# Sixteen-by-sixteen triangle inverses moved from VectorE to GpSimd, with five block transfers per chain in place of eighteen

## The chip, the cores and the metric

The kernel runs on one core of a Trainium2 chip. The metric is the device time of one execution in microseconds (us). Names of engines in the profile: PE is TensorE (matmuls), PEld its weight loads, DVE is VectorE, ACT is ScalarE, POOL is GpSimd, and SP (SPq) is the engine that issues most of the DMAs.

## The reference, cut to what matters

Two layers, each a half-step feed-forward block, a mixing block and another half-step feed-forward block, on 512 tokens of width 1024. The mixing block runs three groups of heads side by side on one projection: attention over a sliding window, RWKV-7 and a short convolution.

```python
proj = hn @ w_mix_in[l]
p_att, p_rwkv, p_conv = jnp.split(proj, [...], axis=-1)
y_att  = sliding_window_sink_attention(p_att, ...)      # 8 query heads, window 128
y_rwkv = rwkv7_time_mix(p_rwkv, ...)                    # 4 heads of 64
y_conv = short_conv_mix(p_conv, conv_w[l])
h = h + (1.0 + gt2) * (jnp.concatenate([y_att, y_rwkv, y_conv], -1) @ w_mix_out[l])

# RWKV-7, one head: a state S of 64 x 64, updated token by token
def step(S, inp):
    r_t, w_t, k_t, v_t, kk_t, a_t = inp
    s_kk = jnp.einsum('bhvk,bhk->bhv', S, kk_t)
    S = (S * w_t[:, :, None, :] - s_kk[..., None] * (kk_t * a_t)[:, :, None, :]
         + v_t[..., None] * k_t[:, :, None, :])
    return S, jnp.einsum('bhvk,bhk->bhv', S, r_t)
```

## The kernel before, in words

**The frame.** A layer is the feed-forward block, the mixing block, the feed-forward block. Weights stream from DRAM; each chunk is split into a high and a low part (a cast on ACT at L101, a subtraction on DVE at L102) and multiplied in three matmuls (L98 in the mixing block). The L98 matmuls of the mixing block, 128x256 each, are the projections in and out. They depend on little else, so they serve as the work that PE does while the small steps of the heads wait.

**The chains.** The four RWKV heads are two chains, `rwkv(0)` and `rwkv(1)`, of two heads each; a chain keeps its two heads on the 128 partitions. It replaces the token loop by chunks of 64 tokens (CH = 64). Each chunk of each head needs the inverse of a unit lower triangular 64x64 matrix, and a chain has 16 of them (2 heads, 8 chunks):

1. PE makes the products `ps_c` from `AR` and `a` (L824), and DVE masks them into the tile `B` in two instructions (L828). `LT`, a part of `B`, holds the transposed triangles.
2. The 16x16 diagonal blocks (BASE = 16, four in each 64x64 block, 64 per chain) are gathered, one block to a partition. This goes through DRAM: one transfer writes `LT` to `dl` (L836), eight read the blocks back into `G` (L846).
3. The blocks are inverted by elimination: GpSimd sets `inv` to the identity (two memsets, L848 and L849), then 15 steps follow, of two DVE instructions each: a product into `elim` (L853) and a subtraction from `inv` (L854), on 64 partitions and 15 to 64 elements per partition. Each instruction needs the result of the one before it.
4. The inverted blocks go back through DRAM: one transfer writes `di` (L856), eight read it into `C` (L859).
5. DVE spreads `C` into the block diagonal tile `T` (L907) and transposes it into `TT` (L908). Two levels of 64x64 matmuls on PE (`ps_x`, `ps_t`, `ps_tt`, L916), with masks and subtractions on DVE between them, join the blocks to the inverse of the whole triangle.
6. The rest of the chain (`ps_w`, `ps_gn`, `ps_o`, `ps_s`, `ps_ys`) uses that inverse and runs the state over the chunks.

Between steps 2 and 5 the chain has work that doesn't need the inverse: products `ps_c` from `AR` and `iP` for the tile `K` (L824, L828), the transposes `ps_vN`, `ps_ta`, `ps_beN`, `ps_kaN` (L867) and `ps_xv` (L893).

**The order of the work.** The projections (`products()`), `rwkv(0)`, `rwkv(1)` and `attention()` are generators. A loop at the end of the mixing block takes one step of each that is alive and pays the L98 matmuls out against it by credits, from three totals that are written by hand: `RWKV_WORK, ATT_WORK, FILL_WORK = 29.8, 15.2, 129.6` (L34); the numbers behind `yield` are the costs. From the program written in this way a scheduler fixes the order of the instructions of each engine before the kernel runs. On the chip each engine takes its list in that order, and an instruction that waits holds up all behind it on the same engine. The DMAs of `dl`, `G`, `di` and `C` are issued by SP, from the same list as the weight loads (`wraw`, L267).

Of the kernel before, what the change touches and what calls it, by code (L numbers as in the profile page):

```python
# [8 lines left out]
F32 = mybir.dt.float32  # L9
# [3 lines left out]
ALU = mybir.AluOpType  # L13
# [3 lines left out]
P = 128  # L17
# [8 lines left out]
NB = T // P  # L26
CH = 64
NC = T // CH
HB = math.exp(-0.5) / 2
BASE = 16  # L30
# [27 lines left out]
def trunk_kernel(ctx, tc, ins, out, layers=L, phases=("ffn1", "mix", "ffn2")):  # L58
    nc = tc.nc
# [10 lines left out]
    dram = ctx.enter_context(tc.tile_pool(name="dram", bufs=1, space=bass.MemoryType.DRAM))  # L70
    tt, stt, ts = nc.vector.tensor_tensor, nc.vector.scalar_tensor_tensor, nc.vector.tensor_scalar
    act, mm = nc.scalar.activation, nc.tensor.matmul

    def E(name="e", dt=F32):
        return sp.tile([P, T], dt, name=name, tag="e", bufs=4)
# [34 lines left out]
    rows = (slice(0, CH), slice(CH, P))  # L110
# [7 lines left out]
    for i in range(KD):  # L118
        t = hp_.tile([P, T], F32, name=f"h{i}")
# [15 lines left out]
    for name, v in (("eps", EPS), ("eps64", 64 * EPS), ("gneps", GN_EPS), ("nhb", -HB)):  # L135
        t = const.tile([P, 1], F32, name=f"v_{name}")
# [71 lines left out]
    def square(i, sl):  # L208
        sq = E("sq")[:, sl]
        act(sq, h[i][:, sl], AF.Square)  # L210
        return sq
# [373 lines left out]
    def mix(l, hn, ss, mp, then, ready):  # L585
# [5 lines left out]
        def pair(name):  # L591
            return rows_of(name != "y4", (name + "H", name + "L"))

        def S(q, name, shape=(P, T)):
            return mp.tile(list(shape), F32, name=f"{name}{q}", tag=f"s{q}", bufs=8)
# [4 lines left out]
        def EQ(q, name):  # L600
            return mp.tile([P, T], F32, name=name, tag=f"e{q}", bufs=2)
# [154 lines left out]
        def rwkv(q):  # L756
# [38 lines left out]
            t = EQ(q, "k2")  # L795
# [36 lines left out]
            B_, other = yield from pairs(be, "B", other)  # L832
            LT = B_[:, :, :, 0]

            dl = dram.tile([P, 2 * NB, CH], F32, name="dl", tag=f"dl{q}", bufs=2)
            nc.sync.dma_start(dl, LT.rearrange("p e b t -> p (e b) t"))  # L836
            NM = CH // BASE
            NT = 2 * NM * 2 * NB
            square = lambda t: t[:NT, : BASE * BASE].rearrange("p (t u) -> p t u", u=BASE)
            G = square(EQ(q, "G"))  # L840
            for c in range(2):
                for m in range(NM):
                    n = (c * NM + m) * 2 * NB
                    p0 = c * CH + m * BASE
                    src = dl[p0 : p0 + BASE, :, m * BASE : (m + 1) * BASE]
                    nc.sync.dma_start(G[n : n + 2 * NB], src.rearrange("r n t -> n r t"))  # L846
            V_ = square(EQ(q, "inv"))
            nc.gpsimd.memset(V_, 0.0)  # L848
            nc.gpsimd.memset(V_.rearrange("p t u -> p (t u)")[:, :: BASE + 1], 1.0)  # L849
            for s in range(BASE - 1):  # L850
                n = BASE - 1 - s
                t = mp.tile([NT, BASE * BASE // 4], F32, name="elim", tag=f"el{q}")[:, : n * (s + 1)].rearrange("p (t u) -> p t u", u=s + 1)
                tt(t, G[:, s, s + 1 :].unsqueeze(2).to_broadcast([NT, n, s + 1]), V_[:, s : s + 1, : s + 1].to_broadcast([NT, n, s + 1]), ALU.mult)  # L853
                tt(V_[:, s + 1 :, : s + 1], V_[:, s + 1 :, : s + 1], t, ALU.subtract)  # L854
            di = dram.tile([2 * NM, 2 * NB, BASE, BASE], F32, name="di", tag=f"di{q}", bufs=2)
            nc.sync.dma_start(di.rearrange("m n t u -> (m n) t u"), V_)  # L856
            C_ = EQ(q, "C")[:, : 2 * NB * BASE].rearrange("p (n u) -> p n u", u=BASE)
            for m in range(2 * NM):
                nc.sync.dma_start(C_[m * BASE : (m + 1) * BASE], di[m].rearrange("n t u -> t n u"))  # L859


            AX = U(q, "AX", [P, 2, NB, 2, CH])
# [80 lines left out]
            with tc.manual_schedule(engines={mybir.EngineType.PE}):  # L943
                for b in range(NB):
                    for c, e in ce:
                        m = mm(pgs[c][rows[e], 0, b], Wn[rows[c], e, b, :CH], beN[rows[c], b, rows[e]], start=True, stop=True)
# [12 lines left out]
            y = S(q, "y")  # L959
            pos = [psum([P, 2, NB, CH], "ps_o", R) for _ in range(2)]  # L960
            with tc.manual_schedule(engines={mybir.EngineType.PE}):
                for b in range(NB):
                    for c, e in ce:
                        m = mm(pos[c][rows[e], 0, b], Wn[rows[c], e, b, :CH], B_[rows[c], e, b, 1], start=True, stop=True)
# [116 lines left out]

        prod = products()
        live, waiting = {}, {"rwkv0": lambda: rwkv(0), "rwkv1": lambda: rwkv(1), "att": attention}
        left, fill, credit = 2 * RWKV_WORK + ATT_WORK, FILL_WORK, 0.0
        more = True
# [28 lines left out]
        for q in range(2):  # L1114
            x = pair("yr")
# [256 lines left out]
```

## Time and profile before

| what | before |
|---|---|
| time, median of 3 runs | 1912.6 us (1911.94 to 1915.08) |
| the profiled execution's own time | 1913.21 us |
| its span in the trace | 1911.2 us |
| mean granted clock of TensorE | 0.996 of full speed |
| PE busy | 1878.8 us of the span |
| DVE busy | 1399.8 us |
| ACT busy | 837.0 us |
| POOL busy | 130.7 us |
| the mixing chains' `dl` transfers issued at | 479.21 and 522.88 us (layer 1), 1415.64 and 1459.31 us (layer 2) |

The profile shows one execution; its own time is 0.6 us over the median. The span is what the trace covers, and 2.0 us of the execution lie around it. In rows of groups the columns are the line, the engine, the operation, the tile written and the tile read, the shapes and the count, then the busy time in us, the mean duration of one in ns and the idle time before them, with what ended it. In rows of the timeline the first number is the start in us and the second the length of the row's work; a bracket at the end is the time that the engine sat idle before it, and what ended that.

### The profile page before, as it was taken

The numbers are of one execution on the slowest core, as the hardware profiler recorded it, in microseconds if no ns is written. First come the engines' busy times: TensorE is split into PE (matmuls) and PEld (weight loads), VectorE is DVE, ScalarE is ACT, GpSimd is POOL, SyncE is SP. The second block draws the span as 40 slices with busy tenths as digits, with TensorE's granted clock in tenths as the row PEclk, the third lists the DMA queues.
The fourth block names the chain that finished last, engine by engine and source line by source line (L and its number), as shares of the span: only waits on it lengthen the run. The fifth ranks groups of instructions, "written<-read, shape, count | busy, mean of one in ns | idle before, by whom it ended". The sixth has DMA issues, their size and how long they took to land. (4 is left out here: it accounts for less than half of the span.)

```text
span 1911.2 us, 37042 instructions
## 1 busy us (share of the span) xinstructions
PE 1878.8 (98%) x15504; PEld 1741.7 (91%) x15504; DVE 1399.8 (73%) x2181; ACT 837.0 (44%) x1264; POOL 130.7 (7%) x212
## 2 busy tenths in 40 slices
PE   8999999999999999999999999999999999999999
PEld 7998899897888999899899989989878899988998
DVE  7687687758976877677877776876599667864862
ACT  4443255346322554155345514544562235532551
POOL 0101100100000001110100020010000000110000
PEclk8999999999999999999999999999999999999999
DMA  7767877521312476887727678781321315774741
GB/s 300 245 168 221 271 198 229 168 70 45 79 43 81 123 198 176 278 218 199 264 62 193 171 260 242 191 278 42 93 61 49 88 34 163 209 217 130 198 140 59
DMA packets 104326, 308.46 MB, mean 161 GB/s; under 512 B 23392, under 2 KB 24416, under 8 KB 103136
## 3 DMA queue, kind: packets, MB, share of 16 engines
q1 hardware_dynamic: 75936, 203.33, 32.9%
q0 software_dynamic: 28224, 102.77, 21.7%
q8 instruction: 121, 1.98, 0.4%
q14 instruction: 45, 0.37, 0.1%
HBM read 302.66 MB, written 3.41 MB: 160 GB/s over the span
## 5 line engine op out<-in xcount | busy, mean ns | idle before, releaser
L101 ACT CAST wH<-wraw 128x1024 fp32r<-128x1024 f32 (+2 forms) x292 | 268.4, 922 | 512.6 <-PE ps_mm L91 176.8
L102 DVE TENSOR_TENSOR wL<-wraw,wH 128x1024 fp32r<-128x1024 f32 (+2 forms) x292 | 308.1, 1058 | 96.9 <-ACT wH L101 95.8
L90 PE MATMUL ps_mm<-actH,wH 128*128 128x512 f32 (+1 forms) x784 | 288.5, 368 | 0.0
L91 PE MATMUL ps_mm<-actL,wH 128*128 128x512 f32 (+1 forms) x784 | 288.0, 367 | 0.0
L92 PE MATMUL ps_mm<-actH,wL 128*128 128x512 f32 (+1 forms) x784 | 288.0, 367 | 0.0
L441 PE MATMUL ps_d<-comH,wH 128*128 128x256 f32 x816 | 226.8, 278 | 1.6 <-ACT wH L101 0.8
L443 PE MATMUL ps_d<-comH,wL 128*128 128x256 f32 x816 | 225.8, 277 | 2.3 <-DVE wL L102 2.3
L442 PE MATMUL ps_d<-comL,wH 128*128 128x256 f32 x816 | 225.5, 276 | 0.0
L98 PE MATMUL ps_mm<-hnH,wH 128*128 128x256 f32 x1040 | 214.0, 286 | 5.1 <-ACT hnH L101 2.9
L98 PE MATMUL ps_mm<-hnL,wH 128*128 128x256 f32 x1040 | 211.8, 283 | 0.0
L98 PE MATMUL ps_mm<-hnH,wL 128*128 128x256 f32 x1040 | 209.5, 281 | 0.5 <-DVE wL L102 0.5
L163 DVE SCALAR_TENSOR_TENSOR wada<-wada,crep 128x1024 f32<-128x1024 f32 x140 | 168.0, 1220 | 47.8 <-DMA wada<-in_wadaT 47.6
L102 DVE TENSOR_TENSOR wL<-sum,wH 128x1024 fp32r<-128x1024 f32 x102 | 124.8, 1224 | 74.9 <-ACT wH L101 74.7
L98 PEld LDWEIGHTS ps_mm<-hnH,wH 128*128 128x128 f32 x1040 | 159.5, 190 | 16.1 <-issue 8.2
L92 PEld LDWEIGHTS ps_mm<-actH,wL 128*128 128x128 f32 x784 | 147.8, 189 | 24.4
L90 PEld LDWEIGHTS ps_mm<-actH,wH 128*128 128x128 f32 x784 | 147.8, 189 | 24.2
L91 PEld LDWEIGHTS ps_mm<-actL,wH 128*128 128x128 f32 x784 | 147.8, 189 | 24.1
L101 ACT CAST wH<-sum 128x1024 fp32r<-128x1024 f32 x102 | 107.5, 1054 | 140.3 <-PE ps_d L442 60.1
L98 PEld LDWEIGHTS ps_mm<-hnL,wH 128*128 128x128 f32 x1040 | 160.2, 190 | 6.7 <-issue 5.7
L98 PEld LDWEIGHTS ps_mm<-hnH,wL 128*128 128x128 f32 x1040 | 160.1, 190 | 4.1 <-issue 2.9
L441 PEld LDWEIGHTS ps_d<-comH,wH 128*128 128x128 f32 x816 | 153.2, 188 | 3.9 <-ACT wH L101 1.4
L443 PEld LDWEIGHTS ps_d<-comH,wL 128*128 128x128 f32 x816 | 153.2, 188 | 2.9 <-DVE wL L102 2.9
(402 smaller groups left out, 4237.3 us busy)
## 6 DMA issues: line engine op xcount, KB each, us to landing
wada<-in_wadaT POOLq DMA_DIRECT2D x128, 512.0 KB, 4.9
wraw<-in_wmi SPq DMA_DIRECT2D x40, 512.0 KB
wraw<-in_w2p SPq DMA_DIRECT2D x36, 512.0 KB
wraw<-in_w1p SPq DMA_DIRECT2D x32, 512.0 KB
wraw<-in_w1o SPq DMA_DIRECT2D x32, 384.0 KB
wraw<-in_w2o SPq DMA_DIRECT2D x32, 384.0 KB
wraw<-in_w1i SPq DMA_DIRECT2D x20, 512.0 KB
wraw<-in_w1o SPq DMA_DIRECT2D x32, 320.0 KB
```

Source lines behind the costliest of these rows:

```text
L90: mm(acc, wH, xH, start=start, stop=False)
L91: mm(acc, wH, xL, start=False, stop=False)
L92: mm(acc, wL, xH, start=False, stop=stop)
L98: mm(acc[:, sl], w[a][:, k], x[b][:, sl], start=start and n == 0 and sl is HALVES[0], stop=stop and n == 2, skip_group_check=True)
L101: nc.scalar.copy(hi, src)
L102: nc.vector.tensor_sub(lo, src, hi.bitcast(F32))
L163: stt(w, w, 1.0, crep, ALU.mult, ALU.mult, accum_out=out_)
L441: mm(pt[:, i], wH, x[k][0], start=start and i + k == 0, stop=False, skip_group_check=True)
L442: mm(pt[:, i], wH, x[k][1], start=False, stop=False, skip_group_check=True)
L443: last = mm(pt[:, i], wL, x[k][0], start=False, stop=k == 3, skip_group_check=True)
```

## The change

The 30 elimination instructions per chain are issued to GpSimd (`nc.gpsimd.tensor_tensor`) in place of DVE; what they compute is the same. The scratch in DRAM is laid out so that fewer transfers do the regrouping. `dl` has one row of 64x64+64 elements per block of 64 by 64, so that the four diagonal blocks of a row lie at one stride: two transfers write it (one per half of the partitions) and one reads all of `G`. `di` is written by one transfer as before, in another order of the blocks, and one transfer reads all of `C`. The sizes of the pieces stay as they were: 1024 pieces of 256 bytes for `dl`, 1024 of 64 bytes for `G` and for `C`, 64 of 1024 bytes for `di`. The function has five lines less afterwards, so that lines from L862 on are five lower in the changed kernel (`ps_x` is at L911 there, `T` at L902).

```diff
-            dl = dram.tile([P, 2 * NB, CH], F32, name="dl", tag=f"dl{q}", bufs=2)
-            nc.sync.dma_start(dl, LT.rearrange("p e b t -> p (e b) t"))
             NM = CH // BASE
-            NT = 2 * NM * 2 * NB
+            NT = 2 * NB * 2 * NM
             square = lambda t: t[:NT, : BASE * BASE].rearrange("p (t u) -> p t u", u=BASE)
+            dl = dram.tile([2 * NB * 2, CH * CH + CH], F32, name="dl", tag=f"dl{q}", bufs=2)
+            for c in range(2):
+                nc.sync.dma_start(dl[:, : CH * CH].rearrange("(n c) (r t) -> c r n t", c=2, t=CH)[c], LT[rows[c]].rearrange("p e b t -> p (e b) t"))
             G = square(EQ(q, "G"))
-            for c in range(2):
-                for m in range(NM):
-                    n = (c * NM + m) * 2 * NB
-                    p0 = c * CH + m * BASE
-                    src = dl[p0 : p0 + BASE, :, m * BASE : (m + 1) * BASE]
-                    nc.sync.dma_start(G[n : n + 2 * NB], src.rearrange("r n t -> n r t"))
+            nc.sync.dma_start(G, dl.rearrange("x (m z) -> (x m) z", m=NM)[:, : BASE * CH].rearrange("y (r t) -> y r t", t=CH)[:, :, :BASE])
             V_ = square(EQ(q, "inv"))
...
             for s in range(BASE - 1):
                 n = BASE - 1 - s
                 t = mp.tile([NT, BASE * BASE // 4], F32, name="elim", tag=f"el{q}")[:, : n * (s + 1)].rearrange("p (t u) -> p t u", u=s + 1)
-                tt(t, G[:, s, s + 1 :].unsqueeze(2).to_broadcast([NT, n, s + 1]), V_[:, s : s + 1, : s + 1].to_broadcast([NT, n, s + 1]), ALU.mult)
-                tt(V_[:, s + 1 :, : s + 1], V_[:, s + 1 :, : s + 1], t, ALU.subtract)
-            di = dram.tile([2 * NM, 2 * NB, BASE, BASE], F32, name="di", tag=f"di{q}", bufs=2)
-            nc.sync.dma_start(di.rearrange("m n t u -> (m n) t u"), V_)
+                nc.gpsimd.tensor_tensor(t, G[:, s, s + 1 :].unsqueeze(2).to_broadcast([NT, n, s + 1]), V_[:, s : s + 1, : s + 1].to_broadcast([NT, n, s + 1]), ALU.mult)
+                nc.gpsimd.tensor_tensor(V_[:, s + 1 :, : s + 1], V_[:, s + 1 :, : s + 1], t, ALU.subtract)
+            di = dram.tile([2 * NB, 2 * NM, BASE, BASE], F32, name="di", tag=f"di{q}", bufs=2)
+            nc.sync.dma_start(di.rearrange("n m t u -> (n m) (t u)"), V_.rearrange("p t u -> p (t u)"))
             C_ = EQ(q, "C")[:, : 2 * NB * BASE].rearrange("p (n u) -> p n u", u=BASE)
-            for m in range(2 * NM):
-                nc.sync.dma_start(C_[m * BASE : (m + 1) * BASE], di[m].rearrange("n t u -> t n u"))
+            nc.sync.dma_start(C_, di.rearrange("n m t u -> (m t) n u"))
```

The scheduler orders every engine anew. On POOL, the list of before at the mixing block of layer 1, between the memsets of a score tile `Sc` and the weight reads of the second feed-forward block, holds nothing but the memsets of `inv` for the two chains:

```order
L1015 MEMSET Sc 128x512 x2
L848 MEMSET inv 64x256
L849 MEMSET inv 64x16
L848 MEMSET inv 64x256
L849 MEMSET inv 64x16
L395 DMA sum_7803<-in_w2p 128x1024
```

The same place in the changed kernel, the first rows:

```order
L1010 MEMSET Sc 128x512 x2
L844 MEMSET inv 64x256
L845 MEMSET inv 64x16
L849 ISA
L849 TENSOR_TENSOR elim<-G,inv 64x15
L850 TENSOR_TENSOR inv<-inv,elim 64x15
L849 TENSOR_TENSOR elim<-G,inv 64x28
L850 TENSOR_TENSOR inv<-inv,elim 64x14x2
L849 TENSOR_TENSOR elim<-G,inv 64x39
L850 TENSOR_TENSOR inv<-inv,elim 64x13x3
```

Thirty `TENSOR_TENSOR` rows per chain stand behind the memsets now, and one `ISA` instruction ahead of the first of them; by its name in the program it reloads the engine's library of operations.

On PE, around the key norm of chain 1 (`ps_kk`, L611), the list of before holds only projection matmuls; its first level product `ps_x` of chain 0 comes 71 rows later, as the row `L916 MATMUL ps_x<-T_5282,B_5115 64x64 x16`:

```order
L98 MATMUL ps_mm<-hnL,wH 128x256 x2
L98 MATMUL ps_mm<-hnH,wL 128x256 x2
L611 MATMUL ps_kk<-kksq,con 128x512
L98 MATMUL ps_mm<-hnH,wH 128x256 x2
```

The same place afterwards (`T_5269` and `B_5115` belong to chain 0, and L911 is the line that was L916):

```order
L98 MATMUL ps_mm<-hnH,wL 128x256
L911 MATMUL ps_x<-T_5269,B_5115 64x64 x16
L98 MATMUL ps_mm<-hnH,wL 128x256
L611 MATMUL ps_kk<-kksq,con 128x512
L98 MATMUL ps_mm<-hnH,wH 128x256 x2
L98 MATMUL ps_mm<-hnL,wH 128x256 x2
L911 MATMUL ps_t<-X_5273,TT_5270 64x64 x16
L911 MATMUL ps_tt<-TT_5270,X_5273 64x64 x16
```

So PE asks for `T` of chain 0 ahead of `ps_kk` of chain 1. In layer 2 it asks for it five projection matmuls behind the attention's last group of `ps_pt` ahead of a block of `ps_av` (L1057 and L1075 before, L1052 and L1070 afterwards), again in the changed list:

```order
L1052 MATMUL ps_pt<-con,Sc 128x128 x4
L98 MATMUL ps_mm<-hnH,wL 128x256
L98 MATMUL ps_mm<-hnH,wH 128x256 x2
L98 MATMUL ps_mm<-hnL,wH 128x256 x2
L911 MATMUL ps_x<-T_15827,B_15673 64x64 x16
L98 MATMUL ps_mm<-hnH,wL 128x256 x2
L1070 MATMUL ps_av<-pmc,V 64x512 x2
```

In the list of before thirteen projection matmuls stand between that `ps_pt` and that `ps_av`, and no `ps_x`. From the last `ps_c<-AR,a` of a chain to its first `ps_x` the list of before counts 249 L98 matmuls for chain 0 of layer 1 and 72 for chain 1, with the levels of chain 0 among those of chain 1. The changed list counts 119 and 97, and for layer 2 88 and 140. For chain 1 of layer 1, beside its 97, the stretch now holds the 16 products of `K`, 16 transposes, 16 `ps_xv`, 10 `ps_s`, 14 `ps_ys`, one `ps_v` and one `ps_g`; for chain 1 of layer 2, beside its 140, the 16 products, 16 transposes and 16 `ps_xv`.

On SP, from the write of `dl` of chain 0 on in layer 1, the list of before (`wraw<-in_wmi` and `wraw<-in_wmo` are weight chunks of the projections in and out):

```order
L836 DMA dl<-B_5115 1024x1x64
L267 DMA wraw<-in_wmi 128x1024
L846 DMA G<-dl 8x16x16 x8
L267 DMA wraw<-in_wmi 128x1024 x2
L998 DMA gw<-in_gw 128x256
L267 DMA wraw<-in_wmi 128x1024
L267 DMA wraw<-in_wmo 128x768
L856 DMA di<-inv 64x256
L859 DMA C<-di 16x8x16 x8
L267 DMA wraw<-in_wmo 128x768
```

and afterwards:

```order
L840 DMA dl<-B_5115 64x8x64 x2
L267 DMA wraw<-in_wmi 128x1024 x2
L842 DMA G<-dl 64x16x16
L267 DMA wraw<-in_wmi 128x1024
L993 DMA gw<-in_gw 128x256
L852 DMA di<-inv 64x256
L854 DMA C<-di 128x8x16
L267 DMA wraw<-in_wmi 128x1024
L267 DMA wraw<-in_wmo 128x768
```

The write of `di`, which waits for the elimination, stands ahead of one `wmi` and one `wmo` chunk that it stood behind.

## The prediction

> **What bounds the kernel now.** I read the page first, for the busy times of the engines.
>
> ```profile
> PE 1878.8 (98%) x15504; PEld 1741.7 (91%) x15504; DVE 1399.8 (73%) x2181; ACT 837.0 (44%) x1264; POOL 130.7 (7%) x212
> ```
>
> PE is busy for 1878.8 of 1911.2 us, so time is won or lost only where PE waits. DVE, from which work is taken, has 27% to spare over the whole run, but that is an average. The windows over the inversion stage of layer 1 come next (columns: window, its length, busy time of PE, PEld, DVE, ACT and POOL, granted clock, DMA share, GB/s).
>
> ```profile
> 480.00:500.00 20.00, 19.23 (x187) 15.31 (x185) 16.81 (x53) 11.10 (x33) 0.00 (x0) 1.00 0.41 102
> 500.00:520.00 20.00, 19.63 (x169) 17.53 (x169) 20.00 (x42) 6.32 (x9) 0.43 (x2) 1.00 0.18 52
> 520.00:540.00 20.00, 18.55 (x441) 16.66 (x435) 18.39 (x49) 3.65 (x7) 0.00 (x0) 1.00 0.26 61
> ```
>
> Here DVE is 84 to 100% busy, GpSimd idle, and PE still busy for 57.4 of 60 us (96%): projection matmuls hide whatever DVE is late with. What leaks through is in the list of waits.
>
> ```profile
> PE ps_bo L611 <- DVE bonus L800: 1.8, 4, 0.6
> PE ps_o L964 <- DVE N L954: 1.2, 2, 0.6
> PE ps_x L916 <- DVE T L907: 1.0, 3, 0.4
> PE ps_c L824 <- DVE B L828: 0.9, 2, 0.5
> ```
>
> These four sum to 4.9 us over both layers. That is the most that a freer DVE can give back through them.
>
> **What is removed from DVE.** Sixty subtractions, and as many products beside them:
>
> ```profile
> L854 DVE TENSOR_TENSOR inv<-inv,elim 64x15 f32<-64x15 f32 (+7 forms) x60 | 11.6, 193 | 1.2
> ```
>
> Twice 11.6 is about 23 us of DVE over the run, 5.8 per chain. They leave a DVE whose lateness costs PE 4.9 us at most; I take 2 us as the gain, since most of those waits are behind instructions with no elimination ahead of them.
>
> **The path of the inverse.** The timeline of chain 1 of layer 1, on SP and on DVE, shows the path in full.
>
> ```profile
> 521.57 1.28 DVE L828 TENSOR_TENSOR B<-ps_c,con 128x512 f32<-128x512 f32 x2
> 522.88 0.55 SPq L836 DMA_DIRECT2D dl<-B  x1
> 526.27 3.61 SPq L846 DMA_DIRECT2D G<-dl  x8
> 532.70 0.16 DVE L853 TENSOR_TENSOR elim<-G,inv 64x15 f32<-64x15 f32 x1
> 540.79 0.17 DVE L854 TENSOR_TENSOR inv<-inv,elim 64x15 f32<-64x15 f32 x1
> 541.02 0.46 SPq L856 DMA_DIRECT2D di<-inv  x1
> 543.93 3.62 SPq L859 DMA_DIRECT2D C<-di  x8
> 549.11 0.69 DVE L907 TENSOR_TENSOR T<-C,con 128x512 f32<-128x512 f32 x1 [0.65 <-DMA C<-di]
> ```
>
> Afterwards I price it, from the end of `B`, as:
> - a second issue of `dl`: 0.6 (0.55 above);
> - write landed, `G` issued: 3.4 above. Chain 0 took 2.97 (rows below), so 3.1;
> - `G` landed: eight issues take 3.61 us, the last starts at 529.43, and the first step runs 3.3 later. One issue: 3.3;
> - 30 steps on GpSimd: X;
> - `di` landed, `C` issued: 2.9 above, 2.1 for chain 0, so 2.6;
> - `C` landed: its last issue starts at 547.1 and `T` starts 2.0 later. One issue with all 1024 pieces is between that and the 5.2 of all eight; I take 2.7, near the lower end, as no issue queue is left;
> - `T` 0.7.
>
> That is 13.0 + X in all. In before, the same path took 27.0 us here (522.85 to 549.80). The 13 saved transfers are worth 3.2 us for `G` and 2.5 for `C` per chain, all of it on this path.
>
> ```profile
> 479.21 0.61 SPq L836 DMA_DIRECT2D dl<-B  x1
> 482.18 2.87 SPq L846 DMA_DIRECT2D G<-dl  x8
> 515.18 0.48 SPq L856 DMA_DIRECT2D di<-inv  x1
> 517.32 4.59 SPq L859 DMA_DIRECT2D C<-di  x8
> ```
>
> Weight chunks that now stand behind `di` on SP (one `wmi`, one `wmo`) are issued when `di` goes. For chain 0 that is X + 7 after 479.2, near 497. The last `wmi` chunk was issued at 509 before, so nothing is late.
>
> **One step on GpSimd.** The trace has no such step. The nearest rows are its memsets:
>
> ```profile
> L1015 POOL MEMSET Sc<- 128x512 f32 x4 | 2.0, 533 | 70.8 <-DVE wL L102 70.8
> L848 POOL MEMSET inv<- 64x256 f32 x4 | 1.2, 304 | 246.7 <-DVE es L1043 153.8 <-DVE k L798 92.9
> L849 POOL MEMSET inv<- 64x16 f32 x4 | 0.5, 120 | 0.2
> 468.92 0.30 POOL L848 MEMSET inv<- 64x256 f32 x1 [76.88 <-DVE es L1043]
> 469.28 0.12 POOL L849 MEMSET inv<- 64x16 f32 x1
> ```
>
> From one memset's start to the next's is 0.36 us, 0.30 of work and 0.06 between. The bounds of a step, from one start to the next: at least 0.12 + 0.06 = 0.18 (a write of 16 elements that reads nothing), at most 0.53 + 0.06 = 0.59 (the 512-element memset). A step writes 15 to 64 elements but reads two operands, and waits for its predecessor's result. I take 0.36, the 256-element row, as 45 elements on average with two reads and a write each are nearer to it than to 16 writes. So X = 30 x 0.36 = 10.8, with ends 5.3 and 17.7. DVE's step in the rows above is 0.28 (532.70 to 540.79 in 29 steps, other work included).
>
> The Trainium skill, GPSIMD Engine Reference, section 4.1 Engine selection, says that a two-input elementwise operation on GpSimd is about twice as slow as on VectorE, and sends such work to VectorE. By it, as an estimate, a step is 2 x 0.193 = 0.39, X is 11.6, and the sum below would be 2.4 us higher. It speaks against this change; no row here shows the operation on GpSimd.
>
> The `ISA` library reload ahead of the first step lies between the memset (469) and the landing of `G` (some 486), 16 us in which GpSimd has nothing else; I cost it at nothing, and its whole length if it comes after `G`.
>
> **What hides the path.** PE asks for `ps_x` where the new list puts it. The rows of PE that fix the deadlines:
>
> ```profile
> 474.80 0.66 PE L824 MATMUL ps_c<-AR,a 64*64 64x128 f32 x14
> 478.51 0.68 DVE L828 TENSOR_TENSOR B<-ps_c,con 128x512 f32<-128x512 f32 x1
> 503.88 1.02 PE L611 MATMUL ps_kk<-kksq,con 128*128 128x512 f32 x2
> 518.11 0.40 PE L98 MATMUL ps_mm<-hnL,wH 128*128 128x256 f32 x2
> 518.35 0.40 PE L98 MATMUL ps_mm<-hnH,wL 128*128 128x256 f32 x2
> 519.48 1.10 PE L824 MATMUL ps_c<-AR,a 64*64 64x128 f32 x32
> 527.81 1.10 PE L916 MATMUL ps_tt<-TT,X 64*64 64x64 f32 x32
> 528.76 1.15 PE L916 MATMUL ps_x<-T,B 64*64 64x64 f32 x32
> 1414.94 0.68 DVE L828 TENSOR_TENSOR B<-ps_c,con 128x512 f32<-128x512 f32 x1
> 1434.51 0.40 PE L98 MATMUL ps_mm<-hnH,wL 128*128 128x256 f32 x2
> 1455.91 1.10 PE L824 MATMUL ps_c<-AR,a 64*64 64x128 f32 x32
> 1458.00 1.27 DVE L828 TENSOR_TENSOR B<-ps_c,con 128x512 f32<-128x512 f32 x2
> ```
>
> - Chain 0, layer 1: `ps_x` now stands just ahead of `ps_kk`, which PE reaches at 503.9. `B` ends at 479.2, so 24.7 us are covered and X may be 11.6. No stall at 10.8.
> - Chain 1, layer 1: 97 projection matmuls at 0.12 (518.35 less 518.11, halved) make 11.4 us. Groups of 16 small products take about 1 us (527.81 to 528.76): `ps_c`, `ps_xv`, `ps_s` and `ps_ys` together some 3.8. The 16 transposes are 1.9 at the same 0.12, and `ps_v` and `ps_g` 1 us each, as `ps_kk` was. Sum 19.0, and with PE 96% busy 19.7. PE leaves `ps_c` at 520.6 and is at `ps_x` at 540.3; `T` is there at 522.85 + 13.0 + X. X may be 4.4, and the stall is 6.4.
> - Chain 0, layer 2: the place of `ps_x` is 1434.5 on the clock of before, `B` ends at 1415.6. X may be 5.9; stall 4.9.
> - Chain 1, layer 2: 140 projection matmuls, 16.4 us, and 3.9 of small work, 21.1 at 96%. PE is there at 1478.1, `B` ends at 1459.3. X may be 5.8; stall 5.0.
>
> A stalled PE also loses clock. Late in the run stands a gap with what follows it:
>
> ```profile
> 1523.00:1526.00 3.00, 1.28 (x12) 1.08 (x10) 1.57 (x3) 1.05 (x1) 0.00 (x0) 1.00 0.11 44
> 1526.00:1530.00 4.00, 3.55 (x21) 3.14 (x21) 2.13 (x4) 1.44 (x3) 0.00 (x0) 0.60 0.54 124
> ```
>
> After 1.7 us of idling the granted clock was 0.60 for 4 us, so 1.6 us of work lost. Three stalls longer than that: 4.8 us.
>
> **The sum.** 6.4 + 4.9 + 5.0 = 16.3 of stalls, 4.8 of clock, less 2 of relief: +19.1 on the profiled execution's 1913.2, that is 1932.3. The median of the runs is 0.6 lower, so 1931.7. In general the stalls are 3X - 16.1, and X - 11.6 more where X is over that. The covers are uncertain downward: without the allowance for waits, and with chain 0's at up to 3 us less as the list moved, 7 us more.
>
> **The rivals.**
> - *GpSimd is quick and DVE's relief decides: faster.* At 0.18 per step X is 5.3, the stalls are under 1 us and no clock is lost; the four waits on DVE give up to 4.9, so 1908 to 1912. It decides below 0.2 per step. For it: DVE's 84 to 100%. Against it: even a memset of 16 elements that reads nothing takes 0.18. Chance 0.05.
> - *Light steps, 0.20 to 0.28.* X 6.0 to 8.4: stalls 2 to 9, clock 0 to 5, +0 to +12. Chance 0.13.
> - *Heavy steps, 0.45 to 0.6.* X 13.5 to 18: stalls 26 to 44, four drops of clock, +30 to +49. Chance 0.18. For it: each step waits for its predecessor on its own engine, which no memset row shows.
> - *GpSimd takes turns with DVE.* If each step had to wait for a DVE instruction to end, 0.48 us each (20.00 us in 42), a step would be 0.84, X 25, the stalls 72 and the time about 1990. The two engines don't overlap in these rows, so nothing excludes it. Chance 0.04. The Trainium skill, SBUF — State Buffer, section Who interferes with whom, has such a lock between a two-input DVE instruction and a GpSimd instruction that reads SBUF; the trace of before has no case of it.
> - *The library reload falls behind `G`,* or waits for something unseen: its length comes on top of X twice at most, some 10 us. Chance 0.02.
>
> That the change doesn't do what it says is excluded by the new list of POOL, which holds all 120 steps, and of SP, which holds five block transfers per chain.
>
> **How the numbers follow.** The forecast, steps of 0.28 to 0.45 (+12 to +31), has 0.58. Its own value is +19. From the 0.05 for faster and the lower third of the light case I leave out 0.09, from the upper part of the heavy case and above it 0.10: the range is +4 to +45 on the median, 1917 to 1958. About 0.2% (3.8 us) is what a measurement of this kernel can tell from no change. Faster by more 0.04; within it 0.07 (the rest of the quick case and the lightest steps); slower 0.89.
>
> **What would show it.** Start-to-start of the GpSimd steps in the POOL timeline: 0.36. PE idle ahead of `ps_x`, with `T` as its releaser, three times at 5 to 6 us and a fourth time at nothing; a granted clock well below 1 right behind. `G` and `C` landing some 3 us behind one issue each. I am wrong if the steps come at 0.2 or less, if `ps_x` doesn't wait, or if PE's loss sits elsewhere, for example at projection matmuls that wait for weight chunks behind `di`.

## The result, and the profile after

The changed kernel takes 1943.67 us (median of 4 runs, 1938.44 to 1947.07), the kernel before 1913.84 (4 runs, 1911.94 to 1917.14). The ratio is 1.0152, with a 95% interval of 1.012 to 1.0184: about 30 us slower, inside the range of the prediction and 12 us above its value. The profiled execution of the changed kernel took 1940.58 us (span 1938.4), 27.4 more than that of before.

The list of waits of PE, after, in the same form as before:

```profile
PE ps_x L911 <- DVE T L902: 20.9, 4, 8.2
PE ps_s L972 <- ACT y L967: 6.2, 4, 2.8
PE ps_bo L611 <- DVE bonus L800: 1.1, 2, 0.6
```

The wait at `ps_x` went from 1.0 to 20.9 us and is now the largest of PE's; of the other DVE waits shown of before, `ps_bo` fell from 1.8 to 1.1, and `ps_o` and `ps_c` are no longer in the list. The wait of `ps_s` on ACT grew to 6.2 from 3.5, which was this row before:

```profile
PE ps_s L977 <- ACT y L972: 3.5, 2, 2.2
```

Three of the four waits at `ps_x` are long. Their rows in PE's timeline (chain 1 of layer 1, then chain 0 and chain 1 of layer 2):

```profile
552.69 1.97 PE L911 MATMUL ps_x<-T,B 64*64 64x64 f32 x32 [4.99 <-DVE T L902]
1448.08 1.97 PE L911 MATMUL ps_x<-T,B 64*64 64x64 f32 x32 [7.60 <-DVE T L902]
1513.97 1.97 PE L911 MATMUL ps_x<-T,B 64*64 64x64 f32 x32 [8.15 <-DVE T L902]
```

The 32 products take 1.97 us each time, where they took 1.15 before: the clock. The windows of the third wait and of what follows (columns as before: length, busy times of PE, PEld, DVE, ACT, POOL, granted clock, DMA share, GB/s):

```profile
1508.00:1514.00 6.00, 0.03 (x2) 0.06 (x3) 0.83 (x2) 0.00 (x0) 0.56 (x3) 0.64 0.33 85
1514.00:1519.00 5.00, 5.00 (x61) 4.66 (x62) 1.26 (x2) 0.00 (x0) 0.00 (x0) 0.50 0.01 2
```

In these 6 us PE does nothing and DVE and POOL next to nothing: what runs is a chain of DMAs. Behind them PE is busy throughout at half its clock. Busy time times the missing share of the clock, summed over windows of 2 us in both mixing blocks, is 8.8 us after and 1.6 before. Over the whole span PE idles 19.5 us more than before and is busy 7.6 us longer, with the same 15504 matmuls: together the 27.2 us by which the span grew.

The path itself, chain 1 of layer 1, on SP, POOL and DVE:

```profile
528.57 1.27 SPq L840 DMA_DIRECT2D dl<-B  x2
532.43 0.60 SPq L842 DMA_DIRECT2D G<-dl  x1
535.84 0.21 POOL L849 TENSOR_TENSOR elim<-G,inv 64x15 f32<-64x15 f32 x1 [17.62 <-DMA G<-dl]
547.39 0.22 POOL L850 TENSOR_TENSOR inv<-inv,elim 64x15 f32<-64x15 f32 x1
547.64 0.47 SPq L852 DMA_DIRECT2D di<-inv  x1
549.57 0.38 SPq L854 DMA_DIRECT2D C<-di  x1
551.85 0.69 DVE L902 TENSOR_TENSOR T<-C,con 128x512 f32<-128x512 f32 x1 [6.95 <-DMA C<-di]
```

The elimination runs from 535.84 to 547.61, 11.8 us; in the other three chains it takes 12.5, 12.3 and 12.4. Before, DVE took 8.3 us here, but 24.8 for chain 0, since there it gave its other work the turn between the steps. The first and the last step of chain 0 before:

```profile
490.36 0.16 DVE L853 TENSOR_TENSOR elim<-G,inv 64x15 f32<-64x15 f32 x1
514.96 0.15 DVE L854 TENSOR_TENSOR inv<-inv,elim 64x15 f32<-64x15 f32 x1
```

So GpSimd halved the elimination of chain 0 and lengthened that of chain 1. Neither length decides by itself: the new list of PE asks for chain 0's result 130 projection matmuls sooner than before.

### The profile page after: what moved, and what is told of

It reads as the page before. It is cut to its first block, busy times and chain, and to the rows that moved or that the text cites. A ratio compares the mean times of both kernels' runs of the same rounds, so it can differ in the third digit from the quotient of the medians.

```text
span 1938.4 us, 36967 instructions
## 1 busy us (share of the span) xinstructions
PE 1886.4 (97%) x15504; PEld 1747.9 (90%) x15504; DVE 1383.1 (71%) x2061; ACT 837.8 (43%) x1264; POOL 171.0 (9%) x332
## 5 line engine op out<-in xcount | busy, mean ns | idle before, releaser
L102 DVE TENSOR_TENSOR wL<-wraw,wH 128x1024 fp32r<-128x1024 f32 (+2 forms) x292 | 308.4, 1059 | 107.9 <-ACT wH L101 106.4
L98 PE MATMUL ps_mm<-hnH,wH 128*128 128x256 f32 x1040 | 214.3, 287 | 5.0 <-ACT hnH L101 2.9
L98 PE MATMUL ps_mm<-hnL,wH 128*128 128x256 f32 x1040 | 213.2, 284 | 0.0
L98 PE MATMUL ps_mm<-hnH,wL 128*128 128x256 f32 x1040 | 211.5, 284 | 0.5 <-DVE wL L102 0.5
L102 DVE TENSOR_TENSOR wL<-sum,wH 128x1024 fp32r<-128x1024 f32 x102 | 124.9, 1224 | 74.3 <-ACT wH L101 74.1
L98 PEld LDWEIGHTS ps_mm<-hnH,wH 128*128 128x128 f32 x1040 | 160.2, 191 | 15.1 <-issue 7.2
L91 PEld LDWEIGHTS ps_mm<-actL,wH 128*128 128x128 f32 x784 | 147.8, 189 | 24.3
L98 PEld LDWEIGHTS ps_mm<-hnL,wH 128*128 128x128 f32 x1040 | 161.5, 191 | 5.9 <-issue 5.2
L98 PEld LDWEIGHTS ps_mm<-hnH,wL 128*128 128x128 f32 x1040 | 160.8, 191 | 5.4 <-issue 3.7
```

What stands on the lines that cost most here:

```text
L91: mm(acc, wH, xL, start=False, stop=False)
L98: mm(acc[:, sl], w[a][:, k], x[b][:, sl], start=start and n == 0 and sl is HALVES[0], stop=stop and n == 2, skip_group_check=True)
L102: nc.vector.tensor_sub(lo, src, hi.bitcast(F32))
```

## The experiments

Theory: PE waits at `ps_x` by the path of the inverse less the work that PE's list puts ahead of `ps_x` (the cover), and loses clock behind each wait. Rivals: the transfers and their layout cost the time; the moved order costs it, whatever GpSimd's speed; GpSimd disturbs VectorE.

**The transfers alone.** The changed kernel with the elimination back on DVE.

```diff
-                nc.gpsimd.tensor_tensor(t, G[...], ...)
-                nc.gpsimd.tensor_tensor(V_[...], ...)
+                tt(t, G[...], ...)
+                tt(V_[...], ...)
```

> Five transfers per chain, elimination on VectorE as before. Theory (the GpSimd steps are what PE waits for): the path of the inverse is some 5 us shorter than before, but before lost only 1.0 us at ps_x, so 1909 to 1915 us, no difference or a few us better. Rival (the new layout in DRAM or the merged transfers cost the time): 1925 us or more.

1915.91 us against 1913.22, ratio 1.0015 (1.0006 to 1.0024): within the 0.2%, and on the slow side of it, just above the span that was expected. By themselves the transfers cost 2.7 of the 30 us at the median. They give nothing: PE's list moved with them (207 and 78 projection matmuls of cover in place of 249 and 72), and the waits are

```profile
PE ps_s L972 <- ACT y L967: 6.7, 4, 2.8
PE ps_x L911 <- DVE T L902: 3.1, 2, 2.0
```

The longer wait of `ps_s` is thus here too, without a step on GpSimd.

**GpSimd alone.** The kernel before, with the elimination on GpSimd and the 18 transfers.

```diff
-                tt(t, G[...], ...)
-                tt(V_[...], ...)
+                nc.gpsimd.tensor_tensor(t, G[...], ...)
+                nc.gpsimd.tensor_tensor(V_[...], ...)
```

> Elimination on GpSimd, the 18 transfers of before. Theory: the path is some 5 us longer than in the changed kernel and the list of PE is made for it only in part (120 and 158 projection matmuls of cover in both layers): four stalls of 5 to 7 us and their clock, 1935 to 1950 us. Rival (the transfers cost the time): 1910 to 1920 us.

1928.04 us, ratio 1.0082 (1.0067 to 1.0098). The direction was right and the size missed: the four stalls were 2.0 to 3.9 us and not 5 to 7. The kernel is slower than before, yet some 15 us faster than the change with both parts. The waits at `ps_x` are

```profile
PE ps_x L916 <- DVE T L907: 12.0, 4, 3.9
```

From the end of `B` to the start of `T` the path took 27.1, 28.8, 29.1 and 28.0 us here and 24.3, 23.3, 25.7 and 23.7 in the changed kernel. The merged transfers save 2.8 to 5.5 us per chain when GpSimd eliminates, and the kernel is slower with them, because the list of PE takes more away. PE came to `ps_x` 25.9, 26.2, 26.0 and 26.1 us behind `B` here, and 24.9, 19.2, 18.9 and 16.4 us behind it in the changed kernel. Part of that are projection matmuls: 158 ahead of chain 1's `ps_x` became 97 and 140 (7.1 and 2.1 us at 0.117), 120 ahead of chain 0's became 88 in layer 2 (3.7 us). The rest are other products that no longer stand there and, for chain 1 of layer 2, a `B` that ends 4.7 us behind its products in place of 1.6. The waits at `ps_x` make 8.9 of the 12.9 us between the two profiled executions. The two parts don't add up: 2.7 us for the transfers and 14.8 for GpSimd are 17.5 of 30, and the rest appears only with both.

**One chain each.** GpSimd for chain 0, DVE for chain 1, five transfers.

```diff
-                nc.gpsimd.tensor_tensor(t, ...)
+                (nc.gpsimd if q == 0 else nc.vector).tensor_tensor(t, ...)
...
```

> Chain 0 on GpSimd, chain 1 on VectorE, five transfers each. Theory: only chain 0 of layer 2 stalls, 7.6 us as in the changed kernel and some 2 of clock, so 1918 to 1925 us; chain 1 has 176 and 179 projection matmuls of cover, over 20 us, for a path that DVE walks in 23, no stall. Rival (contention of the two engines or the moved order costs most): 1930 us or more.

1925.09 us, ratio 1.0062 (1.0048 to 1.0076), at the upper edge of what was expected. One long wait is left, 7.7 us for chain 0 of layer 2, with the same releaser; the other two at `ps_x` are 1.2 and 0.4 us:

```profile
1443.56 1.97 PE L911 MATMUL ps_x<-T,B 64*64 64x64 f32 x32 [7.67 <-DVE T L902]
```

**Seven steps of fifteen.** The strictest test of the moved order: PE's list stays nearly as in the changed kernel, GpSimd's work is cut.

```diff
-            for s in range(BASE - 1):
+            for s in range(7):
```

> The changed kernel with the first 7 of the 15 elimination steps (the other eight are left out, so the blocks are not fully inverted); the list of PE stays nearly that of the changed kernel (119, 97, 86 and 131 projection matmuls of cover). Theory: X falls from 12.2 to about 5.5 us, the four waits at ps_x from 21 us to 0 to 3 us in all, no clock is lost, 1910 to 1918 us. Rival (the moved order itself, or the GpSimd instructions' disturbance of other engines, costs the time): 1928 us or more.

1917.72 us, ratio 1.0021 (1.0012 to 1.0031). The eliminations took 5.7, 4.7, 4.7 and 5.8 us and 25 of the 30 us were gone, with the transfers, nearly the same order and the relieved VectorE all left in place:

```profile
PE ps_s L972 <- ACT y L967: 5.1, 4, 2.1
PE ps_x L911 <- DVE T L902: 3.0, 1, 3.0
```

So nearly all of the moved order's cost arises where the path is longer than its cover. What is left, 4.5 us, is mostly clock: the same sum over windows gives 4.7 us of work lost, against 1.6 before, where the expectation had none, while PE's idle time is 1.2 us above that of before. It also bears on VectorE's relief: 120 instructions on DVE are gone and hardly a stall is left, and no gain on before shows.

**Each product twice.** The other direction.

```diff
                 nc.gpsimd.tensor_tensor(t, G[...], ...)
+                nc.gpsimd.tensor_tensor(t, G[...], ...)
```

> The changed kernel with each product of the elimination issued twice on GpSimd: 45 instructions per chain in place of 30, X longer by 15 x 0.35 = 5.2 us. Covers by the list of PE 122, 110, 97 and 120 projection matmuls. Theory: the four waits at ps_x become about 5, 9, 11 and 16 us (41 in place of 21), so 1958 to 1970 us. Rival (a loss that doesn't hang on the length of the GpSimd work, such as the moved order or the transfers): 1940 to 1950 us.

1951.88 us, ratio 1.0209 (1.0189 to 1.0229). The eliminations grew by 5.2, 5.0, 4.8 and 3.9 us, the waits at `ps_x` from 20.9 to

```profile
PE ps_x L912 <- DVE T L903: 32.3, 4, 9.6
```

The time grew by less than expected (8 us over the changed kernel, not 14 to 26). It lies below the theory's range and 1.9 us above the rival's, so the time alone decides nothing. The waits speak for the theory: they are 4.4, 9.6, 8.9 and 9.4 us, where the changed kernel has 0.2, 5.0, 7.6 and 8.2, and none grew by more than its elimination. They grew less than the path where this kernel's list and `B` gave PE more cover. The largest miss is chain 1 of layer 2, which waits 9.4 us and not 16: `B` comes 1.1 us after its products there and not 4.7, so that PE has 19.9 us of work behind it (1494.57 to 1514.46), where in the changed kernel it has 16.4. A count of matmuls from the products on doesn't show that.

**More cover.** The change as it is, and more projection matmuls ahead of `ps_x`.

```diff
+            yield 2.0
             T_ = S(q, "T", (P, 2, NB, CH))
```

> The changed kernel with one more yield, of cost 2.0, ahead of T, which makes the program pay out more projection matmuls there: the list of PE holds 113, 174, 88 and 186 of them ahead of the four ps_x in place of 119, 97, 88 and 140. Theory (each stall is the path less its cover): the wait of chain 1 falls from 5.0 to 0 us in layer 1 (77 matmuls more, 9.0 us) and from 8.2 to about 2 in layer 2 (46 more and 16 small ones, 6.4 us), that of chain 0 in layer 2 stays 7.6; with two clock drops less, 1925 to 1933 us. Rival (what is moved ahead is missing behind, so nothing is won): 1938 to 1947 us.

1929.82 us, ratio 1.0091 (1.0071 to 1.0111), as the theory had it, but only half for its reason. The waits:

```profile
PE ps_mm L98 <- DVE y L997: 8.3, 2, 4.2
PE ps_x L912 <- DVE T L903: 7.4, 1, 7.4
```

Chain 1 doesn't wait at `ps_x` any more, in either layer. What was moved ahead is then missing at the end of the mixing block: the output projection (L98, reading `yr`) waits 8.3 us for the chains' `y`, a wait that the changed kernel doesn't have. The rival had a part of the truth. The waits add up to less all the same: 13.5 less at `ps_x`, 5.3 less at `ps_s` (6.2 to 0.9), 8.3 more at the end. That is 10.5 us less, of 11.2 between the two profiled executions (13.9 between the medians).

**Shorter subtractions.** In the changed kernel some GpSimd steps take 0.7 to 1.7 us. The rows of POOL and of DVE at one such place, chain 0 of layer 1:

```profile
491.24 0.29 POOL L849 TENSOR_TENSOR elim<-G,inv 64x63 f32<-64x63 f32 x1
491.61 1.39 POOL L850 TENSOR_TENSOR inv<-inv,elim 64x63 f32<-64x63 f32 x1
491.61 1.22 DVE L102 TENSOR_TENSOR wL<-wraw,wH 128x1024 fp32r<-128x1024 f32 x1
493.29 0.69 DVE L1045 TENSOR_TENSOR Sc<-Sc,den 128x512 f32<-128x512 f32 x1
493.44 0.71 POOL L850 TENSOR_TENSOR inv<-inv,elim 64x64 f32<-64x64 f32 x1
494.94 0.69 DVE L1056 TENSOR_TENSOR pmc<-ps_pt,con 128x512 f32<-128x512 f32 x1 [0.95 <-PE ps_pt L1052]
494.99 0.28 POOL L849 TENSOR_TENSOR elim<-G,inv 64x60 f32<-64x60 f32 x1
```

Beside L102 and L1045, which read two tiles in SBUF, the GpSimd step lasts until DVE's is over; beside L1056, which reads one operand from PSUM, it takes its 0.28. All eleven steps of 0.69 us or more in this trace, of 120, overlap a DVE instruction with two operands in SBUF. The experiment cuts L102 of the projection in into four (two of the eight blocks of 128 columns at a time; `l_mix[0]` is set while these weights are fetched).

```diff
-        split(wH[:, :n], wL[:, :n], w[:, :n])
+        nc.scalar.copy(wH[:, :n], w[:, :n])
+        cut = 2 if l_mix[0] else n
+        for k in range(0, n, cut):
+            nc.vector.tensor_sub(wL[:, k : k + cut], w[:, k : k + cut], wH[:, k : k + cut].bitcast(F32))
...
```

> The changed kernel with the weight subtraction of the projection in (VectorE, two operands in SBUF) cut into pieces of 256 columns. In the changed kernel's trace the GpSimd steps that start while such a VectorE instruction runs end with it, up to 1.7 us in place of 0.3. Theory of the lock between the two: the longest step falls to 0.8 us or less and X by about 0.7 us per chain; the time 1936 to 1944 us. Rival (the long steps are something of GpSimd's own): steps of over 1.2 us stay.

1945.26 us, ratio 1.0169 (1.0148 to 1.019): the time missed, the steps came out half as expected. For chain 0 the longest step fell from 1.39 and 1.27 to 0.68 us in both layers, and the elimination from 12.5 and 12.3 to 11.9. Chain 1's grew from 11.8 and 12.4 to 12.2 and 12.8, so that the four together took as long as before. In layer 2, chain 1 has a longer step than any before:

```profile
1498.24 2.29 DVE L272 TENSOR_TENSOR wL<-wraw,wH 128x256 fp32r<-128x256 f32 x5
1498.37 2.23 POOL L855 TENSOR_TENSOR elim<-G,inv 64x15 f32<-64x15 f32 x1 [26.17 <-DMA G<-dl]
```

Five pieces back to back kept GpSimd out for all of their 2.29 us; it didn't get in between them. So a step of over 1.2 us stays, as the rival had it, but it lies under DVE's pieces and is nothing of GpSimd's own. Short instructions are no remedy where they follow each other closely. The time of this kernel can't be laid to the lock alone, since its chain 0 starts 7 us later (second `B` at 486.04, not 478.83).

**Three of four.** GpSimd except for chain 0 of layer 2, with moderate extra cover.

```diff
-                nc.gpsimd.tensor_tensor(t, ...)
+                (nc.vector if (l, q) == (1, 0) else nc.gpsimd).tensor_tensor(t, ...)
...
+            yield ((0, 1.5, 0, 2.0))[2 * l + q]
             T_ = S(q, "T", (P, 2, NB, CH))
```

> GpSimd for three of the four eliminations, VectorE for chain 0 of layer 2, and a yield of 1.5 and of 2.0 ahead of chain 1's T in the two layers; covers 119, 126, 207 and 98 projection matmuls, the last one with the levels of chain 0 beside it. Theory: waits of 0.2, 1.6, 0 and 0 us, no clock lost, 1912 to 1919 us. Rival (GpSimd's disturbance of VectorE costs time of its own): 1925 us or more.

1914.48 us against 1912.36, ratio 1.001 (1.0001 to 1.002): some 2 us, at most 0.2%, as expected. The waits at `ps_x` are 1.4, 1.6 and 1.7 us (0.2, 1.6 and 0 were expected), and no window of the mixing blocks shows a lower clock. Once their path is nearly covered, GpSimd's 90 steps cost no more than that, and gain nothing.

Two more tried for a version that beats the kernel before. **GpSimd in layer 1 only** (a yield of 2.0 for chain 1 there, DVE in layer 2):

> GpSimd for both chains of layer 1, VectorE for both of layer 2, a yield of 2.0 ahead of chain 1's T in layer 1; covers 119, 132, 207 and 78. Theory (GpSimd gains nothing where PE didn't wait before): waits at ps_x of 2 to 5 us in all, 1911 to 1917 us, not faster than before. Rival (a freer VectorE gives time back once the stalls are gone): 1908 us or less.

1916.71 us, ratio 1.0015 (1.0006 to 1.0024), with 4.2 us of waits at `ps_x`: as expected. **Three of four with more cover** (yields of 3.0 and 2.5):

> As the kernel with three eliminations on GpSimd and chain 0 of layer 2 on VectorE, with yields of 3.0 and 2.5 ahead of chain 1's T: covers 119, 150, 207 and 110. Theory: the wait of chain 1 in layer 1 falls from 1.6 us to 0, part of it comes back at the output projection, which then waits for y: 1911 to 1917 us, not faster than before. Rival (a freer VectorE gives time back): 1908 us or less.

1916.87 us, ratio 1.0012 (1.0002 to 1.0022), again as expected. The profiled execution is the fastest of its twelve (1911.09 us), with these waits:

```profile
PE ps_mm L98 <- DVE y L997: 5.2, 2, 3.0
PE ps_x L912 <- DVE T L903: 1.6, 1, 1.6
```

The wait again changes place, from `ps_x` to the end of the block. No version of the change beat the kernel before.

## Why the prediction was right, point by point

**The step on GpSimd.** Forecast 0.36 from the memset row, between 0.18 and 0.59. Measured, the two groups:

```profile
L850 POOL TENSOR_TENSOR inv<-inv,elim 64x15 f32<-64x15 f32 (+7 forms) x60 | 20.7, 345 | 4.7
L849 POOL TENSOR_TENSOR elim<-G,inv 64x15 f32<-64x15 f32 (+7 forms) x60 | 19.1, 319 | 84.6 <-DMA G<-dl 80.3
```

With 0.08 between steps that is 0.41 from start to start. Without the steps that a DVE instruction held up it is 0.35 (chain 0 of layer 1: 12.47 us less 2.0 of holding, over 30). The memset row gave the undisturbed step, and the lock came on top, 1.5 to 2.1 us per chain. X was 11.8 to 12.5, not 10.8. That the row fits is partly luck: a step on 15 elements takes 0.21 us where the memset of 16 takes 0.12, one on 64 takes 0.30 as the memset of 256 does, and no row of before tied the two together. GPSIMD Engine Reference, section 4.1 Engine selection, of the Trainium skill has two-input work at about twice VectorE's time; here the busy time is 332 ns against 190, 1.7 times, with the held-up steps in it, and 1.4 times without them (0.35 less 0.08 is 0.27). The prediction's 2 x 0.193 sets a busy time beside times from start to start: with its 0.06 between instructions that step would be 0.45 and X 13.4.

**The lock** was named as a rival that would make a step 0.84 and X 25. It exists but makes only two or three steps per chain last 0.69 us or more, and does not add 0.48 us to each of the thirty as the rival assumed: the long steps all lie beside DVE instructions with two operands in SBUF. The Trainium skill, SBUF — State Buffer, section Who interferes with whom, says that a DVE instruction with two inputs in SBUF contends with a GpSimd instruction that reads SBUF; the rows at 491 to 495 agree.

**The transfers.** The constant part of the path was put at 13.0 us and was 12.2 for chain 1 of layer 1 (24.0 from the end of `B` at 528.54 to that of `T` at 552.54, less 11.8) and 14.1 for chain 0 of layer 2 (26.4 less 12.3). There the first step ran 4.8 us behind the issue of `G` where 3.3 was forecast. Part of that was there to see before: the prediction split the eight issues evenly and put the last at 529.43, while the trace starts it at 528.77, 3.9 us ahead of the first step. In the kernel with 18 transfers the path was 2.8 to 5.5 us longer; the forecast had 5.7 for `G` and `C` together.

**The stalls.** Forecast 0, 6.4, 4.9 and 5.0, measured 0.2, 5.0, 7.6 and 8.2; the sum 16.3 against 20.9. For chain 1 of layer 1 the path was as forecast (24.0 us, 23.8 forecast) and the cover 19.2 us, not 17.5. For chain 0 of layer 2 the cover was right: PE came to `ps_x` at 1440.5, 18.9 us behind `B`, as worked out from the place in the list, and the whole 2.7 us of error are the path (X and the landing of `G`). For chain 1 of layer 2 most of it is the cover. PE was there 16.4 us behind `B` in place of 18.8, as `B` came late after its products.

**The clock.** Three drops were forecast at 1.6 us each, 4.8. The sum over windows grew by 7.2: behind the three waits PE worked for 4.6, 3.5 and 5.9 us at a clock of 0.50. The forecast took its price from a drop of 3.4 us (1526.8 to 1530.2). The wait ahead of that one was longer than the 1.7 us that fell into the prediction's window; its row before:

```profile
1526.45 0.33 PE L977 MATMUL ps_s<-St,GT 64*64 64x64 f32 x4 [2.17 <-ACT y L972]
```

**The relief of DVE** was put at 2 of 4.9 us. The waits of PE behind DVE instructions in the list of before fell by about 2.8 (`ps_bo`, `ps_o`, `ps_c`), but that of `ps_s` on ACT grew by 2.7, which no step of the prediction had. Neither is shown to come from a freer DVE. With the transfers alone and the elimination still on DVE these three waits fell as far, with 0.5 us of a new one at `ps_o`, and `ps_s` grew by 3.2. So the transfers and the order that comes with them are enough for both. With 19.9 more at `ps_x`, 7.2 of clock and 2.7 at `ps_s`, less 2.8, the account comes to 27.0 of the 27.4 us between the two profiled executions.

So the mechanism was right. The terms that were mis-sized are X (lock left out), the landing of `G` for chain 0 of layer 2, the cover of chain 1 in layer 2, and the clock, all of which made the forecast too low; the cover of chain 1 in layer 1 was off the other way, by 1.7 us. The rivals of quick, light and heavy steps fell with the step's 0.35 to 0.41, and no cost of the library reload was seen: the first step of layer 1 started 0.14 us after `G` had landed and took 0.20 us.

What stays open: why PE's list asks for `T` so much earlier than the path ends. The lists show that it does; by what durations the scheduler placed it was not tried.

## What to carry to other kernels

Work that moves to a free engine can move the order of the others with it, as it did here: compare the lists, and hold the length of the moved path against the cover that the busy engine now has, place by place. An engine that is 84 to 100% busy in a stage is worth relieving only if the bound engine waits for it there; here the four waits that the prediction named came to 4.9 us over both layers, and it isn't shown that any of that was won by the relief. And cover that is moved ahead of one wait is taken from a later one: check what waits last at the end of the stage.

## What the runs showed of the hardware

A GpSimd step on 64 partitions with 15 to 64 elements, where no DVE instruction held it up, takes 0.20 to 0.31 us and the next starts 0.08 later; with 15 elements it is 0.21, so most of it doesn't depend on the size. Back-to-back DVE instructions with two SBUF operands keep a GpSimd instruction out for as long as they follow each other (2.23 us beside five of them).

The clock can fall behind short waits of PE. In the kernel with GpSimd and 18 transfers, a wait of 2.0 us at `ps_x` had 3.4 us at half the clock behind it:

```profile
502.00:507.00 5.00, 2.99 (x23) 2.19 (x24) 2.62 (x4) 1.91 (x2) 0.00 (x0) 1.00 0.13 12
507.00:511.00 4.00, 4.00 (x44) 3.76 (x44) 4.00 (x7) 0.63 (x1) 0.00 (x0) 0.58 0.00 0
```

The length of the wait alone doesn't decide. Waits of 1.5 us at `ps_s` had such a drop behind them in three runs (the transfers alone, one chain each, seven steps). With three of four, waits of 1.4 to 1.7 us lost none, and with the transfers alone neither did waits of 2.05 and 2.84 us. Every wait of 2.9 us or more in the mixing blocks of these runs had a drop of 3.4 to 10.2 us that began within it or right behind it. What decides between 1.4 and 2.9 us stays open.
